# The tail of a one-core trunk kernel: three additions to x by VectorE in place of accumulating DMAs, squares moved behind sigmoids, two rows finished in parts

## The chip, the cores and the metric

The kernel runs on one core of one Trainium2 chip. The time is device microseconds (us) from one launch; lower is better. Five engines matter: TensorE (PE, matmul), VectorE (DVE), ScalarE (ACT), GpSimd (POOL) and SyncE (SP). Each executes its own instructions strictly in the order in which they were written down, and waits at an instruction until the semaphores that it names have been reached. DMAs are issued from SP and from POOL.

## The reference

One layer of a transformer trunk, batch 1, 512 tokens of width 2048, float32:

```python
hn = rmsnorm(x, norm_g[0])
y = swa_mixer(hn, w_in, w_out, sinks, rel_bias)   # windowed attention, gated, times w_out
x = x + y
emb = p[0] @ ple_proj[0]
g = jax.nn.sigmoid(rmsnorm(x, ple_norm[0]) @ ple_gate[0])
x = x + emb * g
return rmsnorm(x, final_g)                        # x * rsqrt(mean(x*x) + eps) * final_g
```

Only the last three lines concern the change: the sigmoid gate, the addition to x, and the final norm over each token's 2048 values.

## The kernel before

**Tiling.** x lies in SBUF as one tile `x1s` of 128 partitions x 4 column pieces j x 4 token rows t x 512, and `x1[j]` is its column piece j. The text names a piece of 128 tokens by 512 columns as (t, j); row t is the four pieces (t, 0) to (t, 3). Each matrix product is done with three float32r matmuls (high by high, low by high, high by low part: `mm3`), and the weights are split into the two parts by ACT (a cast, lines 755 and 763) and DVE (a subtraction, lines 756 and 764). The two large products (by `w_out`, then by `ple_gate`) are done by a two-level scheme of seven block products, worked in the order 1, 7, 6, 5, 3, 4. Product 5 yields the gate inputs of pieces (2, 2), (3, 2), (2, 3), (3, 3); product 3 those of (0, 2), (1, 2) and then (0, 3), (1, 3); the sums of several products those of (0, 0), (1, 0), (0, 1), (1, 1); product 4, which is last, those of (2, 0), (2, 1), (3, 0), (3, 1).

**Per piece** the generator `gated` (line 1381) writes three steps, and the caller decides by `next` and `run` where each lands: (a) a sigmoid on ACT, with the row's first norm as its scale (line 1387); (b) a multiplication by the embedding on DVE (line 1389), then the addition to x, either as a DMA issued from POOL with an add on arrival (line 1393) or as an addition on DVE (line 1395); (c) a square on ACT that also sums the 512 values into `ssq3` (line 1406). Step (c) reads the x that step (b) has made, so after a DMA it waits for that DMA to land.

**Per row**, once its four sums are there, `power_of_mean` makes the row's factor: a reduction and a scaling on DVE, a power on POOL (line 1361). The row is then multiplied by that factor and by the final gain, in one of two ways: in one DVE instruction (`row`, line 1420), or by the gain beforehand on DVE (`by_gain`, line 1412) and by the factor on ACT (line 1609 or 1621). `store` issues the piece's write to HBM from SP (line 1415).

**What sets the order.** For this stretch the order of all five engines is written by hand: the order of calls is the order on each engine. `later`, `moved` and `moves` are lists of steps: at fixed points between matmuls some of `later` is run; `moved` holds step (c) of gates whose DMAs are in flight, to be run at a later point.

**The tail.** `block(jj, tb)` issues the 24 matmuls of product 4 for piece (2 + tb, jj). PE works (2, 0), (2, 1), (3, 0) and then (3, 1) in two column parts of 288 and 224. `two` are the gates of (0, 3) and (1, 3). The last part of (3, 1) is squared and summed in one DVE instruction, row 3's factor follows on POOL, then the last scalings and stores. Tiles in the profile: `g` and `open` are PSUM banks with gate inputs, `s` the gate's scratch, `e` the embedding, `fg` the gain, `yn` the rows' factors.

Of the kernel before, what the change touches and what calls it, by code (L numbers as in the profile page):

```python
# [55 lines left out]
def trunk_kernel(ctx: ExitStack, tc: tile.TileContext, a: dict):  # L56
    nc = tc.nc
# [100 lines left out]
    def run(gen):  # L158
        for _ in gen:
            pass  # L160
# [21 lines left out]
    kinds, g = [], 0  # L182
# [16 lines left out]
    for k in range(KC):  # L199
# [95 lines left out]
        if 3 <= k < 3 + NB:  # L295
            t = k - 3
# [384 lines left out]
    def block(nm, r, c, jj, m):  # L681

        r = r if nm == "w_out" else 3 - r
        return a[nm][2 * (c - 1) + jj, 4 * (r - 1) + m]
# [16 lines left out]
    for nm, p in SUMS:  # L701
        for q in (6, 5) if (nm, p) == ("ple_gate", 5) else (p,):
            sum_small(nm, q)
        for jj in range(2):
            for m in range(4):
                t = summed[nm, p, jj, m] = tc.dram_tile([P, WE], F32, name=f"{nm}_{p}_{jj}_{m}")
# [262 lines left out]
    x1 = [x1s[:, j] for j in range(4)]  # L969
# [335 lines left out]
    for n, p in enumerate(ORDER_OUT):  # L1305
        nxt = out_forms.steps(ORDER_OUT[n + 1]) if n < 5 else iter(())
        for jj in range(2):
# [12 lines left out]
            def todo():  # L1320
                step = next(calls)
                part = x_at.get((p, jj, step))
                if part is not None:
                    load_x(part, nc.sync)
                part = embed_steps.get((p, jj, step))
                if part is not None:
                    embedding.prepare(part)
                next(nxt, None)
                if p == 4:

                    for _ in range({0: 1, 1: 2, 2: 2, 3: 2, 5: 1, 6: 2, 7: 2}.get(4 * jj + step, 0)):
                        turn(*turns.pop(0), "o")
                    if jj:
                        next(ple_first, None)
# [20 lines left out]
    def power_of_mean(out, ssq, nm):  # L1355

        w = out.shape[-1]
        ms = const.tile([P, NB], F32, tag="ms_r", name=f"ms_{nm}")[:, :w]
        nc.vector.tensor_scalar(ms, ssq, 1.0 / D, EPS, op0=ALU.mult, op1=ALU.add)
        yield  # L1360
        nc.gpsimd.tensor_tensor(out, ms, power[:, :w], op=ALU.pow)
# [7 lines left out]
    def load_embeds(c, jj):  # L1369
        t = embed_of[c, jj] = late.tile([P, 2, 512], F32, tag="e", name=f"e{c}_{jj}", bufs=2)  # L1370
        nc.sync.dma_start(t, embeds[c, jj])
# [9 lines left out]
    def gated(t, j, zin, z, e, c=slice(0, 512), share=1.0):  # L1381


        n = done[t]
        done[t] += 1
        xt = x1[j][:, t, c]
        nc.scalar.activation(z, zin, AF.Sigmoid, scale=rstd2[:, t : t + 1])
        yield
        nc.vector.tensor_mul(z, e[:, c], z)
        if t < 3 or j >= 2:  # L1390
            if t < 2 and j < 2:
                yield
            nc.gpsimd.dma_start(xt, z, accum_op=ALU.add)
        else:
            nc.vector.tensor_add(xt, xt, z)
        yield
        if (t, j) == (3, 1) and share != 1.0:
            flat = x1s.rearrange("p j t c -> p (j t c)")
            at = (NB + 3) * 512
            xt = flat[:, at + c.start : at + c.stop + 1]  # L1400
            nc.vector.scalar_tensor_tensor(
                out=s2[:, 1, 1, c.start - 1 : c.stop], in0=xt, scalar=share, in1=xt, op0=ALU.mult, op1=ALU.mult,
                accum_out=ssq3[:, t, n : n + 1],
            )
        else:
            nc.scalar.activation(z, xt, AF.Square, accum_out=ssq3[:, t, n : n + 1])

    def gain(j):
        return fg[:, j * 512 : (j + 1) * 512]

    def by_gain(t, j):
        nc.vector.tensor_mul(x1[j][:, t, :], x1[j][:, t, :], gain(j))

    def store(t, j):
        nc.sync.dma_start(a["out"][t * P : (t + 1) * P, j * 512 : (j + 1) * 512], x1[j][:, t, :])

    def row(t, j, yn):

        xt = x1[j][:, t, :]
        nc.vector.scalar_tensor_tensor(out=xt, in0=xt, scalar=yn, in1=gain(j), op0=ALU.mult, op1=ALU.mult)  # L1420
# [33 lines left out]
    moved, moves = [], []  # L1454
# [14 lines left out]
    opens = {  # L1469
        (3, 1, 0): (0, 0, "t"), (3, 1, 1): (1, 0, "t"), (3, 1, 2): (0, 1, "o"), (3, 1, 3): (1, 1, "o", lower),  # L1470
    }
    gains = {(3, 1, 0): (0, 0), (3, 1, 1): (1, 0), (3, 1, 2): (0, 1), (3, 1, 3): (1, 1)}

    def split_last(k):
        if k % 2 == 0:
# [16 lines left out]
    for n, p in enumerate(ORDER_PLE[:-1]):  # L1492
        if n == 1:

            ctx.enter_context(
                tc.manual_schedule(
                    engines={getattr(mybir.EngineType, v) for v in ("PE", "SP", "DVE", "Activation", "Pool")}
                )
            )
        nxt = ple_forms.steps(ORDER_PLE[n + 1])  # L1500
        for jj in range(2):
            calls = iter(range(4))

            def todo():
                step = next(calls)
                k = early.get((p, jj, step))
                if (p, jj, step) in embed_loads:
                    load_embeds(*embed_loads[p, jj, step])
                while small_due:
                    small_due.pop(0)()  # L1510
                if (p, jj, step) == (5, 0, 2):
                    assert len(moves) == 4
                    while moves:
                        moves.pop(0)()
                if turns:
                    turn(*turns.pop(0), "t")
                    if not turns:
                        nc.vector.tensor_reduce(ss2, ssq2, axis=AX.X, op=ALU.add)
                        run(power_of_mean(rstd2, ss2, "r2"))
                        nc.scalar.activation(ss2[:, :1], ss2[:, :1], AF.Sigmoid)  # L1520
                    return
                next(nxt, None)
                if p == 1:
                    next(nxt, None)
                if k is not None:
                    split_last(k)
                if (p, jj, step) in opens:
                    open_bank(*opens[p, jj, step])
                if (p, jj, step) in gains:
                    by_gain(*gains[p, jj, step])  # L1530

            def between(m, ps):
                if (p, m) == (7, 3):
                    gate(p, jj, ps, None)
                q = ple_steps.get((p, jj, m))
                if q is not None:
                    small_ple.prepare(q)
                for q in SMALL["ple_gate"].get((p, jj), {}).get(m, ()):
                    small_ple.product(q)
                if (p, jj, m) == (6, 1, 1):  # L1540
                    later.append(partial_of(gate_later, "sum", 0, None, embeds_for(1, 0)))

            ps = unit(p, jj, at_ple, ple_forms, todo, between)
            last_two, held_e = (p, jj) == (3, 1), {}
            if not (p == 7 or last_two):
                later.insert(0, partial_of(gate_later, p, jj, ps, held_e))
            for of, which in EMBEDS.get((p, jj), ()):
                e = embeds_for(of, which)
                held_e.update(e)
                if of == 1:  # L1550
                    later.insert(1, partial_of(gate_later, "sum", which, None, dict(e)))
                    held_e.clear()
            if p == 5 or (p, jj) == (3, 0):
                while moved:
                    later.extend(moved.pop(0))
        run(nxt)
# [21 lines left out]
    two = gate(3, 1, ps, e)  # L1578
# [1 line left out]
        for g in two:  # L1580
            next(g)
    load_embeds(4, 1)
    for step in moved.pop():
        step()
    yn2 = const.tile([P, 3], F32, name="yn2")
    ssum = const.tile([P, 3], F32, name="ssum")
    nc.gpsimd.memset(power[:, 3:], 0.5)
    first = block(0, 0)
    next(first)
    next(first)  # L1590
    for t in (2, 3):
        for j in (2, 3):
            by_gain(t, j)
    for g in two:
        run(g)
    nc.vector.tensor_reduce(ssum[:, :2], ssq3[:, :2, :4], axis=AX.X, op=ALU.add)
    root = power_of_mean(yn2[:, :2], ssum[:, :2], "r3")
    next(root)
    run(root)
    g = block(1, 0)  # L1600
    next(g)
    next(g)
    run(first)
    for t in range(2):
        for j in (2, 3):
            row(t, j, yn2[:, t : t + 1])
            store(t, j)
        for j in range(2):
            nc.scalar.mul(x1[j][:, t, :], x1[j][:, t, :], yn2[:, t : t + 1])
            store(t, j)  # L1610
    run(g)
    nc.vector.tensor_reduce(ssum[:, 2:], ssq3[:, 2, :4], axis=AX.X, op=ALU.add)
    root = power_of_mean(yn2[:, 2:], ssum[:, 2:], "r4")
    next(root)
    run(root)
    g = block(0, 1)
    next(g)
    next(g)

    def scaled_row(j):  # L1620
        nc.scalar.mul(x1[j][:, 2, :], x1[j][:, 2, :], yn2[:, 2:])

    scaled_row(2)
    for j in range(2):
        row(2, j, yn2[:, 2:])
    for j in (2, 0, 1):
        store(2, j)
    run(g)

    base, yn = (const.tile([P, 1], F32, name=f"{v}_3") for v in ("base", "yn"))  # L1630
    g = block(1, 1, lower)
    next(g)
    scaled_row(3)
    store(2, 3)
    next(g)
    by_gain(3, 0)
    run(g)
# [82 lines left out]
```

## Time and profile before

| | us |
|---|---|
| median of 3 runs (791.64 to 792.34) | 791.79 |
| the profiled execution's own time | 791.74 |
| its span, first to last instruction | 790.0 |
| PE busy | 777.2 (98%) |
| DVE busy | 609.0 (77%) |
| ACT busy | 525.7 (67%) |
| POOL busy | 151.6 (19%) |

The span is what the trace covers; 1.74 us of the profiled execution lie outside it. Busy shares are means over the whole span; the change touches only about its last 40 us, so those are read from the timeline there. In the timeline a row has the start in us, the duration in us, the engine, the line, the operation, output and input with their sizes, how many equal instructions were merged into it, and, in brackets, how long the engine was idle before it and what it was waiting for.

### The profile page before, as it was taken

The page shows a single profiled execution, that of the slowest core. Times are in us where ns is not written, and L with a number is a line of the kernel's source. Part 1 is how long each engine was busy: PE and PEld are TensorE (multiplying, and loading weights), DVE is VectorE, ACT ScalarE, POOL GpSimd, SP SyncE. Part 2 cuts the span into 40 slices and gives each one's busy share as a digit, 9 for nine tenths or more (in the row PEclk, how much of TensorE's full clock was granted, in tenths as well). Part 3 has the DMA queues.
Part 4 walks back from the last instruction along what each step waited for, and adds up shares of the span by engine and source line. Part 5 has one row for each costly group of instructions (what it writes and reads, how often), then busy time and mean ns, then how long its engine had stood idle before and what let it go on. Part 6 is the DMA issues. An engine that isn't in the chain of part 4 may idle for free. (4 is left out here: it accounts for less than half of the span.)

```text
span 790.0 us, 11176 instructions
## 1 busy us (share of the span) xinstructions
PE 777.2 (98%) x3708; PEld 649.5 (82%) x3708; DVE 609.0 (77%) x1046; ACT 525.7 (67%) x1105; POOL 151.6 (19%) x276
## 2 busy tenths in 40 slices
PE   9999999999999999999999999999999999999993
PEld 8888888888888888888888888888888888888783
DVE  4547697876878687877777898975897849998975
ACT  6743576666767586766666754568778967665964
POOL 0201423132223323122222200011000002221121
PEclk9999999999999999999999999999999999999997
DMA  9988899999999989999997489767797289999956
GB/s 345 279 219 297 190 277 300 296 276 266 279 264 273 264 232 316 236 306 263 274 268 192 137 319 356 238 239 243 263 391 251 80 322 277 271 274 323 262 121 226
DMA packets 50825, 207.51 MB, mean 263 GB/s; under 512 B 7552, under 2 KB 8576, under 8 KB 45008
## 3 DMA queue, kind: packets, MB, share of 16 engines
q1 hardware_dynamic: 39152, 154.58, 55.7%
q0 software_dynamic: 11616, 52.23, 32.9%
q8 instruction: 29, 0.48, 0.2%
q14 instruction: 28, 0.23, 0.1%
HBM read 192.31 MB, written 75.55 MB: 339 GB/s over the span
## 5 line engine op out<-in xcount | busy, mean ns | idle before, releaser
L756 DVE TENSOR_TENSOR blo<-braw,bhi 128x1024 fp32r<-128x1024 f32 x100 | 121.9, 1222 | 31.1 <-ACT bhi L755 30.2
L755 ACT CAST bhi<-braw 128x1024 fp32r<-128x1024 f32 x100 | 104.9, 1049 | 38.6 <-PE o L128 13.9
L126 PE MATMUL gps<-xh,whi 128*128 128x512 f32 x256 | 100.0, 390 | 0.0
L127 PE MATMUL gps<-xl,whi 128*128 128x512 f32 x256 | 99.9, 390 | 0.0
L128 PE MATMUL gps<-xh,wlo 128*128 128x512 f32 x256 | 99.7, 390 | 0.0
L126 PE MATMUL qps<-xh,whi 128*128 128x512 f32 x224 | 87.8, 392 | 0.0
L127 PE MATMUL qps<-xl,whi 128*128 128x512 f32 x224 | 87.4, 390 | 0.0
L128 PE MATMUL qps<-xh,wlo 128*128 128x512 f32 x224 | 87.3, 390 | 0.0
L570 POOL TENSOR_SCALAR_AFFINE_SELECT own<-r 64x512 fp32r<-64x512 f32 (+1 forms) x48 | 32.5, 676 | 243.4 <-DVE r L560 240.9
L110 DVE TENSOR_TENSOR wlo<-wraw,whi 128x1024 fp32r<-128x1024 f32 x60 | 73.5, 1226 | 3.4 <-ACT whi L109 3.2
L127 PE MATMUL o<-blo,fho 128*128 128x512 f32 x192 | 74.9, 390 | 0.0
L126 PE MATMUL o<-bhi,fho 128*128 128x512 f32 x192 | 74.8, 390 | 0.0
L128 PE MATMUL o<-bhi,flo 128*128 128x512 f32 x192 | 74.8, 389 | 0.0
L556 ACT CAST r<-pt 128x256 fp32r<-128x256 f32 x64 | 23.9, 374 | 68.9 <-PE pt L551 68.7
L109 ACT CAST whi<-wraw 128x1024 fp32r<-128x1024 f32 x60 | 62.3, 1040 | 5.2 <-issue 4.1
L126 PE MATMUL g<-bhi,fhg 128*128 128x512 f32 x160 | 62.8, 392 | 0.0
L127 PE MATMUL g<-blo,fhg 128*128 128x512 f32 x160 | 62.5, 391 | 0.0
L128 PE MATMUL g<-bhi,flg 128*128 128x512 f32 x160 | 62.3, 390 | 0.0
L128 PEld LDWEIGHTS gps<-xh,wlo 128*128 128x128 f32 x256 | 48.1, 188 | 10.3
L126 PEld LDWEIGHTS gps<-xh,whi 128*128 128x128 f32 x256 | 48.1, 188 | 9.1
L529 ACT ACTIVATE t<-t,sm 128x129 f32<-128x129 f32 (+1 forms) x128 | 49.6, 390 | 8.7 <-DVE sm L525 7.4
L560 DVE TENSOR_TENSOR r<-pt,r 128x256 fp32r<-128x256 f32 x56 | 23.7, 424 | 41.1 <-ACT r L556 40.4
(288 smaller groups left out, 1833.8 us busy)
## 6 DMA issues: line engine op xcount, KB each, us to landing
wraw<-in_w_gate_in SPq DMA_DIRECT2D x32, 512.0 KB, 7.9
w_out<-in_w_out POOLq DMA_DIRECT2D x32, 512.0 KB, 9.0
braw<-w_out SPq DMA_DIRECT2D x32, 512.0 KB, 5.2
wraw<-in_w_q SPq DMA_DIRECT2D x28, 512.0 KB, 6.6
braw<-in_w_out SPq DMA_DIRECT2D x22, 512.0 KB, 4.7
braw<-in_ple_gate SPq DMA_DIRECT2D x22, 512.0 KB, 6.5
xw<-in_first SPq DMA_DIRECT2D x14, 640.5 KB, 6.5
w_out<-in_w_out SPq DMA_DIRECT2D x16, 512.0 KB, 10.5
```

Of the source, the lines that this page charges most:

```text
L109: nc.scalar.copy(hi, raw)
L110: nc.vector.tensor_sub(lo, raw, hi.bitcast(F32))
L126: nc.tensor.matmul(ps, sh, mh, start=first, stop=False, skip_group_check=more)
L127: nc.tensor.matmul(ps, sh, ml, start=False, stop=False, skip_group_check=more)
L128: nc.tensor.matmul(ps, sl, mh, start=False, stop=last, skip_group_check=more)
L529: nc.scalar.activation(su, su, AF.Exp, bias=sm[:, u : u + 1], accum_out=sm[:, 2 + u : 3 + u])
L556: nc.scalar.copy(rh, src)
L560: nc.vector.tensor_sub(rl, src, rh.bitcast(F32))
L570: nc.gpsimd.affine_select(out=flat(own), in_=flat(r).bitcast(F32), pattern=[[0, 8], [sign, HB]], compare_op=ALU.is_ge, fill=0.0, base=-HB ...
L755: nc.scalar.copy(hi[:, :n], raw)
L756: nc.vector.tensor_sub(lo[:, :n], raw, hi[:, :n].bitcast(F32))
```

## The change

Nothing before the end of product 5 is touched, and PE's instructions are the same in the same order.

- Pieces (0, 3), (1, 3) and (2, 1) are added to x by DVE instead of a DMA from POOL. (3, 0) and (3, 1) were already added by DVE; (0, 2), (1, 2) and (2, 0) stay with the DMA.
- The squares of (2, 3) and (3, 3) are no longer run among the casts during product 3's second half, and the squares of (0, 2) and (1, 2) no longer before the sigmoid of (2, 0). The former are now behind the sigmoids of (0, 3) and (1, 3), the latter behind the sigmoid of (2, 0). The square of (2, 0) is now behind the sigmoid of (2, 1).
- The four multiplications by the gain of (0, 0), (1, 0), (0, 1), (1, 1) no longer stand among the weight splits of product 3 but in the tail; those of (2, 2), (2, 3) and of (3, 2), (3, 3) stand behind the row factors' reductions.
- Rows 0 and 1 are multiplied and stored in two parts, row 0 before row 1, around the second and third `block`; row 2's pieces (2, 2) and (2, 3) are multiplied by ACT after the third.

The core of the diff:

```diff
@@ gated
-        if t < 3 or j >= 2:
+        if (t >= 2) == (j >= 2) or (t, j) in ((0, 2), (1, 2), (2, 0)):
@@ loop over product 3
-    gains = {(3, 1, 0): (0, 0), (3, 1, 1): (1, 0), (3, 1, 2): (0, 1), (3, 1, 3): (1, 1)}
...
-                if (p, jj, step) in gains:
-                    by_gain(*gains[p, jj, step])
...
-            if p == 5 or (p, jj) == (3, 0):
+            if p == 5:
                 while moved:
                     later.extend(moved.pop(0))
@@ tail
-    for step in moved.pop():
+    for step in moved.pop(0):
         step()
...
+    def rows_by_gain(t):
+        for j in (2, 3):
+            row(t, j, yn2[:, t : t + 1])
+            store(t, j)
+
+    def rows_by_root(t, js):
+        for j in js:
+            nc.scalar.mul(x1[j][:, t, :], x1[j][:, t, :], yn2[:, t : t + 1])
+            store(t, j)
+
+    run(two[0])
+    by_gain(0, 0)
     first = block(0, 0)
     next(first)
     next(first)
-    for t in (2, 3):
-        for j in (2, 3):
-            by_gain(t, j)
-    for g in two:
-        run(g)
+    run(two[1])
+    for step in moved.pop(0):
+        step()
+    assert not moved
+    for t, j in ((1, 0), (0, 1), (1, 1)):
+        by_gain(t, j)
     nc.vector.tensor_reduce(ssum[:, :2], ssq3[:, :2, :4], axis=AX.X, op=ALU.add)
     root = power_of_mean(yn2[:, :2], ssum[:, :2], "r3")
     next(root)
     run(root)
+    for j in (2, 3):
+        by_gain(2, j)
     g = block(1, 0)
     next(g)
+    rows_by_gain(0)
     next(g)
+    rows_by_root(0, range(2))
+    rows_by_gain(1)
     run(first)
-    for t in range(2):
-        for j in (2, 3):
-            row(t, j, yn2[:, t : t + 1])
-            store(t, j)
-        for j in range(2):
-            nc.scalar.mul(x1[j][:, t, :], x1[j][:, t, :], yn2[:, t : t + 1])
-            store(t, j)
     run(g)
+    rows_by_root(1, range(2))
     nc.vector.tensor_reduce(ssum[:, 2:], ssq3[:, 2, :4], axis=AX.X, op=ALU.add)
     root = power_of_mean(yn2[:, 2:], ssum[:, 2:], "r4")
     next(root)
     run(root)
+    for j in (2, 3):
+        by_gain(3, j)
+    for j in range(2):
+        row(2, j, yn2[:, 2:])
+        store(2, j)
     g = block(0, 1)
     next(g)
     next(g)
-
-    def scaled_row(j):
-        nc.scalar.mul(x1[j][:, 2, :], x1[j][:, 2, :], yn2[:, 2:])
-
-    scaled_row(2)
-    for j in range(2):
-        row(2, j, yn2[:, 2:])
-    for j in (2, 0, 1):
-        store(2, j)
+    rows_by_root(2, (2, 3))
     run(g)
...
     g = block(1, 1, lower)
     next(g)
-    scaled_row(3)
-    store(2, 3)
     next(g)
     by_gain(3, 0)
     run(g)
```

What that makes of the instruction streams is seen best at two places. The first is ACT from the sigmoids of (0, 3) and (1, 3) to the sigmoid of (3, 0). Line 1387 is a sigmoid, and the bank it reads names the piece: `open0_0`, `open1_0`, `open0_1` are (2, 0), (2, 1), (3, 0), and `g1_1_0`, `g1_1_1` are (0, 3), (1, 3). Line 1406 is a square; a wait for DMASW is a wait for one of POOL's DMAs to land, one for DVE, PE or Pool is for that engine. Lines 1609 and 1593 multiply by a row factor. Before:

```order
L1406 ACTIVATE s1_5036,ssq3_5035<-x1s_5033 128x512 [waits DMASW1_49,DVE_49]
L1406 ACTIVATE s1_5036,ssq3_5035<-x1s_5033 128x512 [waits DMASW2_49,DVE_49]
L1387 ACTIVATE s2_5037<-open0_0_0_7687,rstd2_6603 128x512 [waits PE_49]
L1406 ACTIVATE s1_5036,ssq3_5035<-x1s_5033 128x512 [waits DMASW3_49,DVE_49]
L1406 ACTIVATE s1_5036,ssq3_5035<-x1s_5033 128x512 [waits DMASW4_49,DVE_49]
L1387 ACTIVATE s2_5037<-open1_0_0_7714,rstd2_6603 128x512 [waits PE_49,Activation_49]
L1406 ACTIVATE s2_5037,ssq3_5035<-x1s_5033 128x512 [waits DMASW5_49,DVE_49]
L1609 ACTIVATE x1s_5033<-x1s_5033,yn2_7777 128x512 [waits Pool_49]
L1609 ACTIVATE x1s_5033<-x1s_5033,yn2_7777 128x512 x3
L1406 ACTIVATE s2_5037,ssq3_5035<-x1s_5033 128x512 [waits DMASW6_49,DVE_49]
L1387 ACTIVATE s2_5037<-open0_1_0_7736,rstd2_6603 128x512 [waits PE_49,Activation_49]
```

The six squares are those of (0, 2), (1, 2), then (0, 3), (1, 3), then (2, 0), then (2, 1); the sigmoids of (2, 0), (2, 1) and (3, 0) stand behind two, two and one wait for a DMA. Now:

```order
L1406 ACTIVATE s7_5038,ssq3_5035<-x1s_5033 128x512 [waits DMASW7_49]
L1406 ACTIVATE s7_5038,ssq3_5035<-x1s_5033 128x512 [waits DMASW0_49]
L1406 ACTIVATE s1_5036,ssq3_5035<-x1s_5033 128x512 [waits DVE_49]
L1387 ACTIVATE s2_5037<-open0_0_0_7687,rstd2_6603 128x512 [waits PE_49]
L1406 ACTIVATE s1_5036,ssq3_5035<-x1s_5033 128x512 [waits DVE_49]
L1406 ACTIVATE s1_5036,ssq3_5035<-x1s_5033 128x512 [waits DMASW1_49]
L1406 ACTIVATE s1_5036,ssq3_5035<-x1s_5033 128x512 [waits DMASW2_49]
L1387 ACTIVATE s2_5037<-open1_0_0_7713,rstd2_6603 128x512 [waits PE_49,Activation_49]
L1593 ACTIVATE x1s_5033<-x1s_5033,yn2_7771 128x512 [waits Pool_49]
L1593 ACTIVATE x1s_5033<-x1s_5033,yn2_7771 128x512 [waits DVE_49]
L1406 ACTIVATE s2_5037,ssq3_5035<-x1s_5033 128x512 [waits DMASW3_49]
L1406 ACTIVATE s2_5037,ssq3_5035<-x1s_5033 128x512 [waits DVE_49]
```

The squares are those of (2, 3), (3, 3), (0, 3), then behind the sigmoid (1, 3), (0, 2), (1, 2), then behind the next sigmoid and row 0's two multiplications (2, 0) and (2, 1). Two multiplications of row 1 and the sigmoid of (3, 0) follow.

The second place is DVE from the last weight split (line 764) to the second row factor's reduction. Line 1412 is a multiplication by the gain, 1420 a row piece by factor and gain, 1395 an addition to x. Before:

```order
L764 TENSOR_TENSOR low7_7762<-grown93_6975,last6_7755 128x1024 [waits DMASW0_49,DVE_49,Activation_49]
L1389 TENSOR_TENSOR s1_5036<-e3_1_7708,s1_5036 128x512 [waits DMAHW5_49,Activation_49]
L1389 TENSOR_TENSOR s1_5036<-e3_1_7708,s1_5036 128x512 [waits Activation_49]
L1389 TENSOR_TENSOR s2_5037<-e4_0_7753,s2_5037 128x512 [waits DMAHW6_49,Activation_49]
L1412 TENSOR_TENSOR x1s_5033<-x1s_5033,fg_6241 128x512 [waits DMASW5_49]
L1412 TENSOR_TENSOR x1s_5033<-x1s_5033,fg_6241 128x512 [waits DMASW7_49]
L1412 TENSOR_TENSOR x1s_5033<-x1s_5033,fg_6241 128x512 [waits DMASW6_49]
L1412 TENSOR_TENSOR x1s_5033<-x1s_5033,fg_6241 128x512 [waits DMASW0_49]
L1596 TENSOR_REDUCE ssum_7778<-ssq3_5035 128x2 [waits Activation_49]
L1359 TENSOR_SCALAR ms_r3_7814<-ssum_7778 128x2 [waits DVE_49,Pool_49]
L1389 TENSOR_TENSOR s2_5037<-e4_1_7773,s2_5037 128x512 [waits DMAHW7_49,Activation_49]
```

Now:

```order
L764 TENSOR_TENSOR low7_7756<-grown93_6975,last6_7750 128x1024 [waits DMASW0_49,DVE_49,Activation_49]
L1389 TENSOR_TENSOR s1_5036<-e3_1_7707,s1_5036 128x512 [waits DMAHW5_49,Activation_49]
L1395 TENSOR_TENSOR x1s_5033<-x1s_5033,s1_5036 128x512 [waits DVE_49]
L1389 TENSOR_TENSOR s1_5036<-e3_1_7707,s1_5036 128x512 [waits Activation_49]
L1395 TENSOR_TENSOR x1s_5033<-x1s_5033,s1_5036 128x512 [waits DVE_49]
L1412 TENSOR_TENSOR x1s_5033<-x1s_5033,fg_6241 128x512 [waits DMASW1_49]
L1389 TENSOR_TENSOR s2_5037<-e4_0_7748,s2_5037 128x512 [waits DMAHW6_49,Activation_49]
L1412 TENSOR_TENSOR x1s_5033<-x1s_5033,fg_6241 128x512 [waits DMASW2_49]
L1412 TENSOR_TENSOR x1s_5033<-x1s_5033,fg_6241 128x512 [waits DMASW3_49]
L1412 TENSOR_TENSOR x1s_5033<-x1s_5033,fg_6241 128x512 [waits DMASW4_49]
L1607 TENSOR_REDUCE ssum_7772<-ssq3_5035 128x2 [waits Activation_49]
L1359 TENSOR_SCALAR ms_r3_7810<-ssum_7772 128x2 [waits DVE_49,Pool_49]
```

Two additions and four multiplications by the gain (one, then three) now stand between the last weight split and the reduction, where four others stood, and no multiplication by the gain stands among the weight splits any more. On POOL the DMAs of (0, 3), (1, 3) and (2, 1) are gone from between the others.

## The prediction

> Times are us from the span's start in the profiled execution before.
>
> **What bounds the kernel now.** I read the busy table by windows first, then the timeline of PE, then ACT's waits, and last the chain of waits, which here needs care.
>
> ```profile
> 760.00:770.00 10.00, 10.00 (x46) 8.29 (x45) 5.33 (x10) 4.03 (x11) 2.70 (x5) 1.00 0.87 176
> 761.02 0.39 PE L128 MATMUL open<-last,flg 128*128 128x512 f32 x1
> 766.46 0.39 PE L128 MATMUL open<-last,flg 128*128 128x512 f32 x1
> 771.90 0.39 PE L128 MATMUL open<-last,flg 128*128 128x512 f32 x1
> 775.15 0.30 PE L128 MATMUL open<-last,flg 128*128 128x288 f32 x1
> 777.84 0.27 PE L128 MATMUL open<-last,flg 128*128 128x224 f32 x1
> ```
>
> In the window PE is busy all the 10 us at full clock (the second number and the 1.00). The five PE rows are the last matmuls of (2, 0), (2, 1), (3, 0) and of the two parts of (3, 1): they end at 761.41, 766.85, 772.29, 775.45 and 778.11, and PE is then done. The span is 790.0, so 11.9 us follow. The sigmoids that wait for these ends start much later:
>
> ```profile
> 763.75 0.67 ACT L1387 ACTIVATE s<-open,rstd 128x512 f32<-128x512 f32 x1
> 767.38 0.63 ACT L1406 ACTIVATE s<-x1s 128x512 f32<-128x512 f32 x1 [2.96 <-DMA x1s<-s]
> 768.71 0.63 ACT L1406 ACTIVATE s<-x1s 128x512 f32<-128x512 f32 x1 [0.61 <-DMA x1s<-s]
> 769.34 0.67 ACT L1387 ACTIVATE s<-open,rstd 128x512 f32<-128x512 f32 x1
> 775.90 0.63 ACT L1406 ACTIVATE s<-x1s 128x512 f32<-128x512 f32 x1 [2.59 <-DMA x1s<-s]
> 776.53 0.67 ACT L1387 ACTIVATE s<-open,rstd 128x512 f32<-128x512 f32 x1
> 779.32 0.48 ACT L1387 ACTIVATE s<-open,rstd 128x288 f32<-128x288 f32 x1
> 780.87 0.44 ACT L1406 ACTIVATE s<-x1s 128x288 f32<-128x288 f32 x1 [0.46 <-DVE x1s L1395]
> 781.32 0.43 ACT L1387 ACTIVATE s<-open,rstd 128x224 f32<-128x224 f32 x1
> ACT s L1406 <- DMA x1s<-s: 9.2, 5, 3.0
> ```
>
> The five sigmoids (L1387) come 2.34, 2.49, 4.24, 3.87 and 3.21 behind their matmuls. Ahead of each of the first three stands a square (L1406) that waits for a DMA to land: ACT is idle 9.2 us in five such waits (last row: total, times, longest). The delay then runs in a ring: late sigmoid, late multiplication, late DMA, late square, next sigmoid late.
>
> ```profile
> 777.66 4.27 issue
> 782.07 0.38 DVE L1389 TENSOR_TENSOR s<-e,s 128x224 f32<-128x224 f32 x1
> ```
>
> The chain of waits doesn't name this: it begins with 4.27 us of "issue" on POOL, time for which it found no releaser. What ends last is the upper part of (3, 1): sigmoid 781.32, multiplication 782.07, and from there 7.93 to the end. PE would have allowed that sigmoid at 778.15:
>
> ```profile
> 707.38 0.39 PE L128 MATMUL g<-bhi,flg 128*128 128x512 f32 x1
> 707.81 1.05 ACT L755 CAST bhi<-braw 128x1024 fp32r<-128x1024 f32 x1 [1.67 <-PE g L128]
> ```
>
> where ACT waits for PE, it starts 0.04 after the matmul's end. So the most that reordering can win is what lies between 778.15 and 781.32, and a little on DVE.
>
> **Part 1: the weight splits.** Four multiplications by the gain leave DVE and two squares leave ACT from before the last splits.
>
> ```profile
> 751.32 0.68 DVE L1412 TENSOR_TENSOR x1s<-x1s,fg 128x512 f32<-128x512 f32 x1
> 759.48 1.21 DVE L764 TENSOR_TENSOR low<-grown,last 128x1024 fp32r<-128x1024 f32 x1
> 760.61 1.28 DVE L1389 TENSOR_TENSOR s<-e,s 128x512 f32<-128x512 f32 x2
> 758.13 1.25 ACT L1387 ACTIVATE s<-g,rstd 128x512 f32<-128x512 f32 x2
> 765.06 2.49 DVE L1412 TENSOR_TENSOR x1s<-x1s,fg 128x512 f32<-128x512 f32 x4
> 770.75 2.74 DVE L1420 SCALAR_TENSOR_TENSOR x1s<-x1s,yn,fg 128x512 f32<-128x512 f32 x4
> 777.24 0.69 DVE L1389 TENSOR_TENSOR s<-e,s 128x512 f32<-128x512 f32 x1 [0.23 <-ACT s L1387]
> 777.96 0.69 DVE L1395 TENSOR_TENSOR x1s<-x1s,s 128x512 f32<-128x512 f32 x1
> ```
>
> Instructions overlap a little: four gains take 2.49, so 0.60 each behind one another; four row pieces 2.74, so 0.67; an addition that needs the multiplication before it starts 0.72 after it. DVE reaches the multiplication of (0, 3) 4 x 0.60 = 2.4 earlier, 758.2. ACT saves two squares of 0.63, sigmoids at about 756.9. PE gets its splits earlier, never later; as it has no gap to close, that is worth nothing in itself.
>
> **Part 2: (0, 3) and (1, 3) on DVE.** Two multiplications, two additions and one gain from 758.2: 0.72, 0.60, 0.72, 0.60, 0.69, free at 761.5. ACT does the deferred squares of (2, 3), (3, 3) (landed long before) and that of (0, 3) by 760.3 and is free for the sigmoid of (2, 0) at 761.45, where it was at 763.75.
>
> **Part 3: the one DMA that still matters.** The multiplication of (2, 0) runs 762.15 to 762.85.
>
> ```profile
> 764.45 0.69 DVE L1389 TENSOR_TENSOR s<-e,s 128x512 f32<-128x512 f32 x1 [2.56 <-ACT s L1387]
> 765.68 0.85 POOL L1393 DMA_DIRECT2D x1s<-s  x1 [2.25 <-issue]
> DMA to landing us min/median/max: 4.2/4.2/4.2
> DMA to landing us min/median/max: 4.2/5.9/6.7
> DMA to landing us min/median/max: 4.0/6.0/10.5
> 763.12 0.63 ACT L1406 ACTIVATE s<-x1s 128x512 f32<-128x512 f32 x1 [0.54 <-DMA x1s<-s]
> ```
>
> The same DMA now starts 0.54 after its multiplication's end, so 763.4 then. The three landing rows are for this one DMA, for the six of the tail, for all fourteen of this line. I take 4.2, its own row: 767.6. The bounds are 4.0 and 10.5. The last row is the square of (1, 2), whose data landed at 763.1; its DMA is issued no later now, and its square comes third behind the sigmoid of (2, 0), at 763.3. No wait.
>
> **Part 4: rows 0 and 1.** Behind the multiplication of (2, 0) DVE does three gains, to 764.6.
>
> ```profile
> 776.66 0.16 DVE L1612 TENSOR_REDUCE ssum<-ssq 128x1 f32<-128x4 f32 x1 [3.17 <-ACT s L1406]
> 777.09 0.56 POOL L1361 TENSOR_TENSOR yn<-ms_r,power 128x1 f32<-128x1 f32 x1 [4.91 <-DVE ms_r L1359]
> ```
>
> From reduction to the end of the power is 0.99: factors at 765.6, where DVE has two gains to do anyway, to 766.2, then two pieces of row 0 to 767.5. The sigmoid of (2, 1) is due at 766.89 and ends at 767.56 (was 769.34); multiplication 767.6, addition 768.3 to 769.0, two pieces of row 1 to 770.25. ACT: row 0's multiplications to 768.8, square of (2, 0) there (landed 767.6), square of (2, 1) 769.4 to 770.15. Reduction at 770.25, gains to 771.8 (the factor is there at 771.3), two pieces of row 2 to 773.1.
>
> ```profile
> 761.92 0.32 SPq L1371 DMA_DIRECT2D e<-embeds  x1
> DMA to landing us min/median/max: 2.4/3.5/4.8
> ```
>
> On SP the last embedding's load (first row) waits for the multiplication of (1, 3), so it goes out at 760.2 and has 7.4 until the multiplication of (2, 1). Behind it come the stores, in the order in which rows are now finished, from about 767 on, each 256 KB and landed within 2.4 to 4.8 (second row, all fourteen). Nothing on another engine waits for a store except POOL's power ahead of the last square, which overwrites one value of the stored (0, 2): it has 10 us.
>
> **Part 5: row 3.** The sigmoid of (3, 0) runs 772.33 to 773.0; its multiplication waits for DVE till 773.1, addition 773.8 to 774.5, square to 775.15. The lower sigmoid is due at 775.49: 0.34 spare. Before, 1.55 passed from it to its square (779.32, 780.87) and 0.45 more to the upper sigmoid: square 777.04, ACT free 777.5, upper sigmoid at PE's 778.15. Its multiplication follows 0.43 + 0.04 later, 778.62; DVE's work between the lower square and that point took 1.20 (780.87 to 782.07), so it is free at 778.24: 0.38 spare.
>
> **Sum.** 782.07 - 778.62 = 3.45 earlier; the 7.93 behind it are the same instructions and transfers. Profiled 791.74 - 3.45 = 788.29; the median of the runs is 0.05 above the profiled execution: 788.3.
>
> DVE costs nothing extra as long as the spare 0.34 + 0.38 = 0.72 and the waits for sigmoids cover it: three additions (2.1) and four gains (2.4) come in, against 2.4 earlier and 2.56 of waiting that it had at 764.45. Without that cover each further us of DVE would be a us at the end.
>
> **A rule against it.** POOL's power now runs beside gains on DVE:
>
> ```profile
> 769.99 0.72 POOL L1361 TENSOR_TENSOR yn<-ms_r,power 128x2 f32<-128x2 f32 x1 [3.46 <-DVE ms_r L1359]
> 770.04 0.69 DVE L1389 TENSOR_TENSOR s<-e,s 128x512 f32<-128x512 f32 x1
> ```
>
> The two ran together before, and DVE's 0.69 is its usual 0.69. If they excluded each other, each of the two factors would come one gain later and push the next gain by the power's 0.6: 0.7 twice, 1.4 in all on DVE, less the spare 0.72: 0.7 lost. The Trainium skill ("SBUF — State Buffer", "Who interferes with whom") says just this: a VectorE instruction with two SBUF inputs and a GpSimd instruction that reads SBUF exclude each other, and the second waits for the first's end. By that rule the time is 789.0; the pair of rows above speaks against it.
>
> **Rivals.** *Exclusion on POOL and DVE*, as priced: 789.0. For it: both factors stand beside gains. Against it: the rows at 769.99 and 770.04.
>
> *The DMA of (2, 0) lands late*, and ACT, in order, holds row 1, the sigmoids of (3, 0) and (3, 1) behind its square. It is needed at 768.8, and with 0.1 at the reduction and the spare 0.72 nothing is lost up to 769.6, 6.2 after its start. At 6.7 it costs 0.5: 788.8. At 9.65 the whole gain is gone. At 10.5 the kernel is slower than before: 773.9 - 769.6 - 3.45 = 0.85, 792.6. For it: one of the fourteen took that long, and new stores start at 767. Against it: by itself it took 4.2, and the six of the tail never above 6.7.
>
> *Another end.* What I don't see, an output transfer or a wait that holds the end where it is: 791.8.
>
> **How the numbers follow.** My forecast 0.74 (its own range 787.4 to 789.2, as the last transfers may land up to a us sooner or later, by the range of the stores); exclusion 0.09; late DMA 0.12, of which 0.05 still faster by over 0.2% (1.6 us, about what a measurement here tells from no change), 0.04 within it, 0.03 slower; another end 0.05, 0.02 within and 0.03 slower. Faster 0.88, same 0.06, slower 0.06. Range 787.4 to 790.3: a late DMA of up to 8.2 is inside.
>
> **What would show it.** Right: the five sigmoids of line 1387 within 0.1 of 761.45, 766.9, 772.3, 775.5, 778.15; no wait of ACT on a DMA from 755 on; PE unchanged to its end. Wrong: a wait before the square of (2, 0); the upper sigmoid behind 778.4 with DVE busy without a gap before it; a power on POOL above 1 us; or the sigmoids on time and more than 7.93 behind the last multiplication.

## The result, and the profile after

The changed kernel takes 787.99 us (median of 6 runs, 787.38 to 788.25), the kernel before beside it 791.68 (6 runs, 791.07 to 792.34): 0.9953 of the time, with a 95% interval of 0.9940 to 0.9966, or 3.7 us less. The profiled execution took 788.25 with a span of 786.5, where 790.0 - 3.45 = 786.55 was forecast.

First the line of busy times of the changed kernel's page, and from its table of windows the stretch from 760 to 770 (length, then busy time and count of PE, weight loads, DVE, ACT, POOL, then PE's clock, share of the DMA engines, GB/s):

```profile
PE 777.0 (99%) x3708; PEld 649.9 (83%) x3708; DVE 611.3 (78%) x1049; ACT 525.5 (67%) x1105; POOL 150.3 (19%) x273
760.00:770.00 10.00, 10.00 (x46) 8.29 (x45) 9.37 (x17) 6.16 (x17) 1.95 (x2) 1.00 0.63 168
```

PE is as full as before. DVE went from 5.33 (10 instructions) to 9.37 (17) in this stretch and ACT from 4.03 (11) to 6.16 (17), since they stand still less and work of the rows that came after 770 now falls in it, on DVE additions and gains too; the DMA engines went from 0.87 to 0.63. The five sigmoids and the squares of (2, 0) and (3, 0), from the timeline of ACT, with the row of ACT's waits that now stands where the 9.2 us on DMAs stood, and PE's last matmul:

```profile
761.32 0.69 ACT L1387 ACTIVATE s<-open,rstd 128x512 f32<-128x512 f32 x1 [0.86 <-PE open L128]
766.82 0.69 ACT L1387 ACTIVATE s<-open,rstd 128x512 f32<-128x512 f32 x1 [2.98 <-PE open L128]
768.64 0.62 ACT L1406 ACTIVATE s<-x1s 128x512 f32<-128x512 f32 x1
772.26 0.69 ACT L1387 ACTIVATE s<-open,rstd 128x512 f32<-128x512 f32 x1 [1.07 <-PE open L128]
774.44 0.63 ACT L1406 ACTIVATE s<-x1s 128x512 f32<-128x512 f32 x1 [0.27 <-DVE x1s L1395]
775.42 0.50 ACT L1387 ACTIVATE s<-open,rstd 128x288 f32<-128x288 f32 x1 [0.26 <-PE open L128]
778.09 0.45 ACT L1387 ACTIVATE s<-open,rstd 128x224 f32<-128x224 f32 x1 [0.61 <-PE open L128]
ACT s L1387 <- PE open L128: 5.8, 5, 3.0
777.72 0.27 PE L128 MATMUL open<-last,flg 128*128 128x224 f32 x1
```

Each of the five now waits for PE and for nothing else (brackets: idle time before it, and what ended it), and the square of (2, 0) at 768.64 follows without a wait. The rest of the tail, from the timelines of DVE and POOL and the view of this one DMA:

```profile
762.05 0.69 DVE L1389 TENSOR_TENSOR s<-e,s 128x512 f32<-128x512 f32 x1 [0.41 <-ACT s L1387]
763.27 0.86 POOL L1393 DMA_DIRECT2D x1s<-s  x1 [6.08 <-issue]
DMA to landing us min/median/max: 3.4/3.4/3.4
764.80 1.29 DVE L1412 TENSOR_TENSOR x1s<-x1s,fg 128x512 f32<-128x512 f32 x2
764.98 1.09 POOL L1361 TENSOR_TENSOR yn<-ms_r,power 128x2 f32<-128x2 f32 x1 [0.85 <-DVE ms_r L1359]
770.47 1.28 DVE L1412 TENSOR_TENSOR x1s<-x1s,fg 128x512 f32<-128x512 f32 x2
770.63 0.92 POOL L1361 TENSOR_TENSOR yn<-ms_r,power 128x1 f32<-128x1 f32 x1 [4.56 <-DVE ms_r L1359]
778.57 0.39 DVE L1389 TENSOR_TENSOR s<-e,s 128x224 f32<-128x224 f32 x1 [0.35 <-ACT s L1387]
```

The last multiplication starts at 778.57 (before: 782.07), and 786.5 - 778.57 = 7.93 follow, as before; in all thirteen profiles of this document it is between 7.89 and 7.98, though the first store starts at 771.53 before and at 766.88 in the change. So neither the earlier stores nor another end is what the gain hangs on. PE's end moves from execution to execution: its last matmul started between 776.85 and 778.08 in the profiles below. So I compare the *tail*, the span less the start of that matmul: 790.0 - 777.84 = 12.16 before, 786.5 - 777.72 = 8.78 after. Spans are printed to a tenth, so a tail is good to about 0.05.

### The profile page after: what moved, and what is told of

The parts are those of the page before. It is cut to its first block, busy times and chain, and to the rows that moved or that the text cites. A ratio compares the mean times of both kernels' runs of the same rounds, so it can differ in the third digit from the quotient of the medians.

```text
span 786.5 us, 11166 instructions
## 1 busy us (share of the span) xinstructions
PE 777.0 (99%) x3708; PEld 649.9 (83%) x3708; DVE 611.3 (78%) x1049; ACT 525.5 (67%) x1105; POOL 150.3 (19%) x273
## 4 chain that ended last, share of the span: by engine, by line
PE 93%; DMA 2%; DVE 1%; issue 1%; ACT 1%; POOL 0%; POOLq 0%; DVEq 0%; ACTq 0%
PE gps L126 7%; PE gps L127 7%; PE gps L128 7%; PE qps L126 7%; PE qps L127 7%; PE qps L128 7%; PE o L127 6%; PE o L126 6%; PE o L128 6%; PE g L127 3%; PE g L128 3%; PE g L126 3%; DMA braw<-ple_gate 2%; PE s L485 2%; PE vps L290 2%; PE pt L551 2%
```

## The experiments

Every run has a kernel before beside it on the same chip; its median was 791.65 beside the first four, 792.13 beside the next four, 791.44 beside the last three.

| kernel | median us (runs) | ratio to before, 95% interval | tail |
|---|---|---|---|
| before | 791.68 (6) | 1 | 12.16 |
| the change | 787.99 (6) | 0.9953, 0.9940 to 0.9966 | 8.78 |
| e1 the additions alone | 788.18 (4) | 0.9956, 0.9941 to 0.9971 | 8.75 |
| e2 the order alone | 797.59 (4) | 1.0071, 1.0056 to 1.0086 | 18.12 |
| e3 gains early again | 787.69 (4) | 0.9951, 0.9936 to 0.9966 | 8.79 |
| e4 squares early again | 788.61 (5) | 0.9962, 0.9948 to 0.9976 | 9.32 |
| e5 one more on DVE | 787.90 (4) | 0.9943, 0.9928 to 0.9958 | 8.75 |
| e6 three more on DVE | 788.98 (4) | 0.9958, 0.9943 to 0.9973 | 10.02 |
| e7 no DMA left | 788.12 (4) | 0.9947, 0.9932 to 0.9962 | 8.79 |
| e8 the DMA of (2, 0) late | 790.98 (10) | 0.9987, 0.9977 to 0.9996 | 11.91 |
| e9 gains ahead of the reductions | 788.07 (3) | 0.9957, 0.9941 to 0.9973 | 9.39 |
| e10 before, (2, 1) on DVE | 788.76 (5) | 0.9971, 0.9957 to 0.9985 | 9.58 |
| e11 before, (0, 3), (1, 3) on DVE | 788.42 (4) | 0.9963, 0.9948 to 0.9978 | 8.86 |

The intervals are about 1.2 us to each side, so medians tell apart only before, e2, e8 and the rest. Differences of some tenths among the rest are read from tails, of one profiled execution each; the five kernels in which the last sigmoid waits for PE (the change, e1, e3, e5, e7) lie between 8.75 and 8.79.

**e1, the additions alone.** The kernel before, with the change's condition and nothing else of it:

```diff
-        if t < 3 or j >= 2:
+        if (t >= 2) == (j >= 2) or (t, j) in ((0, 2), (1, 2), (2, 0)):
```

> The kernel before with one line of the change: (0, 3), (1, 3) and (2, 1) are added by VectorE, all orders as before. Theory (ScalarE's in-order waits for landing DMAs form a ring, and the end follows the upper sigmoid of (3, 1)): the squares of (0, 2), (1, 2) still hold the sigmoid of (2, 0) to about 763.7, but those of (0, 3), (1, 3) and (2, 1) wait for nothing; only the square of (2, 0) waits, to about 770, and row 0's and 1's four multiplications stand behind it. Upper sigmoid about 778.6, its multiplication about 779.3, 2.8 us faster than before, about 0.75 slower than the change. Rival A (the shares of the parts simply add up, additions and order about half each): 1.7 faster. Rival B (the earlier output stores are what counts): no difference from before.

It took the whole gain: tail 8.75, where I had expected 0.75 more than the change. Its stores are issued in the order of before, so their new order is not what counts. From its timelines of ACT and POOL, and its waits:

```profile
763.26 0.67 ACT L1387 ACTIVATE s<-open,rstd 128x512 f32<-128x512 f32 x1
765.19 0.86 POOL L1393 DMA_DIRECT2D x1s<-s  x1 [7.78 <-issue]
768.56 0.63 ACT L1406 ACTIVATE s<-x1s 128x512 f32<-128x512 f32 x1 [1.11 <-DMA x1s<-s]
772.26 0.67 ACT L1387 ACTIVATE s<-open,rstd 128x512 f32<-128x512 f32 x1
778.02 0.45 ACT L1387 ACTIVATE s<-open,rstd 128x224 f32<-128x224 f32 x1 [0.62 <-PE open L128]
ACT s L1406 <- DMA x1s<-s: 3.8, 3, 2.1
```

Three waits on DMAs, 3.8 us, are still there, and the sigmoid of (2, 0) is nearly 2 us later than in the change. Yet the last sigmoid waits for PE: the DMA of (2, 0) starts 1.9 later but lands 3.4 behind its start, and ACT does the square when the change does, at 768.56. The lateness is gone before the end.

**e2, the order alone.** The change with the old condition:

```diff
-        if (t >= 2) == (j >= 2) or (t, j) in ((0, 2), (1, 2), (2, 0)):
+        if t < 3 or j >= 2:
```

> The change with its additions undone: its whole order, but (0, 3), (1, 3) and (2, 1) added by DMAs again. Theory: the square of (0, 3) now stands ahead of the sigmoid of (2, 0) and waits for its DMA to about 764, and that of (2, 1) stands ahead of row 1's multiplications and of the sigmoid of (3, 0) and waits to about 776; upper multiplication about 784, 1 to 3 us SLOWER than before. Rival A (shares add up): 1.7 faster than before. Rival B (stores): faster by most of 3.5.

It is slower than before, by about 6 us. Its timelines of POOL and ACT, and its waits:

```profile
759.65 1.74 POOL L1393 DMA_DIRECT2D x1s<-s  x2 [2.20 <-DVE s L1389]
766.21 0.63 ACT L1406 ACTIVATE s<-x1s 128x512 f32<-128x512 f32 x1 [7.09 <-DMA x1s<-s]
766.84 0.67 ACT L1387 ACTIVATE s<-open,rstd 128x512 f32<-128x512 f32 x1
774.67 0.90 POOL L1393 DMA_DIRECT2D x1s<-s  x1 [2.59 <-issue]
779.95 0.63 ACT L1406 ACTIVATE s<-x1s 128x512 f32<-128x512 f32 x1 [5.90 <-DMA x1s<-s]
781.80 0.67 ACT L1387 ACTIVATE s<-open,rstd 128x512 f32<-128x512 f32 x1
ACT s L1406 <- DMA x1s<-s: 13.9, 3, 7.1
```

The moved squares cannot help: the one left ahead of the sigmoid of (2, 0) is that of (0, 3), whose DMA starts only at 759.65 and lands 6.5 later. ACT stands 7.09, the last 4.5 of it with the sigmoid due (PE's last matmul of (2, 0) ended at 761.65). That sigmoid is 5 us late (766.84), so the later DMA starts at 774.67 and its square holds the next sigmoid until 781.80. Two long waits and one of 0.96 stand in place of five shorter ones, and each feeds the next.

**e3 and e4, one move undone at a time.** In e3 the four gains go back among product 3's splits; in e4 the squares of (2, 3), (3, 3) go back among the casts and those of (0, 2), (1, 2) ahead of the sigmoid of (2, 0). The core of e3, then of e4:

```diff
+                if (p, jj, step) in gains:
+                    by_gain(*gains[p, jj, step])
...
-    by_gain(0, 0)
...
-    for t, j in ((1, 0), (0, 1), (1, 1)):
-        by_gain(t, j)
```

> The change with the four multiplications by the gain of (0, 0), (1, 0), (0, 1), (1, 1) back among the weight splits. Theory: the multiplication of (0, 3) is 2.4 later on VectorE (760.7), the sigmoid of (2, 0) about 1.3 later because the square of (0, 3) stands ahead of it, but three gains fewer follow, so VectorE is about 0.7 late at the multiplication of (3, 0), and its spare time there (0.6) swallows that: within 0.2 us of the change. Rival (clearing VectorE's queue among the splits is a part of the gain by itself): 1 to 2.4 us slower than the change.

```diff
-            if p == 5:
+            if p == 5 or (p, jj) == (3, 0):
...
     run(two[1])
-    for step in moved.pop(0):
-        step()
```

> The change with its four moved squares back: (2, 3), (3, 3) among the casts, (0, 2), (1, 2) ahead of the sigmoid of (2, 0). Theory: the sigmoid of (2, 0) starts at about 762.5 in place of 761.3, VectorE is 1.2 late from there, less its spare 0.6: about 0.6 us slower than the change, still 2.9 faster than before. Rival A (shares add up): the squares carry 1 us or more. Rival C (squares that wait for nothing cost nothing wherever they stand): no difference from the change.

The move of the gains is worth nothing (8.79). The move of the squares is worth 9.32 - 8.78 = 0.54 within the change's order, though e1 does as well without it. In e4 the sigmoid of (2, 0) is late again, behind two squares that wait 1.5 for their DMAs. The lateness reaches the end, since DVE has the four gains in its tail and runs without a gap from 763.13 to 775.36; the last sigmoid follows ACT's work and not PE:

```profile
762.43 0.67 ACT L1387 ACTIVATE s<-open,rstd 128x512 f32<-128x512 f32 x1
777.97 0.43 ACT L1387 ACTIVATE s<-open,rstd 128x224 f32<-128x224 f32 x1
```

PE's last matmul started at 777.38 there, so this sigmoid was due at about 777.7.

**e5, e6 and e7: how much room DVE has.** e5 and e6 add one and three multiplications into scratch behind row 1's pieces by the gain; e7 takes the last DMA away too.

```diff
     rows_by_gain(1)
+    for _ in range(3):
+        nc.vector.tensor_mul(s7[:, 0, 0], gain(0), gain(1))
```

> The change with one more VectorE multiplication of 128x512 (0.60 us, into scratch) behind row 1's two pieces, where VectorE waits for nothing until the multiplication of (3, 0). The tail is measured from the start of PE's last matmul to the end of the span: 8.78 in the change. Theory (spare time of 0.61 on VectorE up to the upper multiplication): no cost, tail 8.8, sigmoid of (3, 1) lower up to 0.3 later. Rival D (VectorE is the bound now, its 0.94 busy share in 760 to 770 says so): 0.6 us slower, tail 9.4.

> The same with three such multiplications, 1.8 us. Theory: 1.8 less the spare 0.61, 1.2 us slower than the change, tail 10.0. Rival D: 1.8 slower, tail 10.6. Rival E (PE sets the end with room to spare): tail 8.8.

```diff
-        if (t >= 2) == (j >= 2) or (t, j) in ((0, 2), (1, 2), (2, 0)):
+        if (t >= 2) == (j >= 2) or (t, j) in ((0, 2), (1, 2)):
```

> The change with (2, 0) added by VectorE too, so that no DMA is left in the tail. Theory: the DMA of (2, 0) lands before its square is due, so nothing is gained, and the addition costs VectorE 0.7 behind the multiplication of (2, 0), which its spare time takes but for 0.1: tail 8.8 to 8.9. Rival (each addition taken from a DMA is worth about a third of 3.4): tail 7.6.

From e5's timelines of DVE and ACT:

```profile
769.34 0.68 DVE L1620 TENSOR_TENSOR s<-fg 128x512 f32<-128x512 f32 x1
769.95 0.15 DVE L1624 TENSOR_REDUCE ssum<-ssq 128x1 f32<-128x4 f32 x1
777.22 0.45 ACT L1387 ACTIVATE s<-open,rstd 128x224 f32<-128x224 f32 x1 [0.39 <-PE open L128]
```

and from e6's:

```profile
770.16 2.14 DVE L1620 TENSOR_TENSOR s<-fg 128x512 f32<-128x512 f32 x3
772.22 0.15 DVE L1624 TENSOR_REDUCE ssum<-ssq 128x1 f32<-128x4 f32 x1
776.45 0.63 ACT L1406 ACTIVATE s<-x1s 128x512 f32<-128x512 f32 x1 [1.51 <-DVE x1s L1395]
777.08 0.48 ACT L1387 ACTIVATE s<-open,rstd 128x288 f32<-128x288 f32 x1
779.02 0.43 ACT L1387 ACTIVATE s<-open,rstd 128x224 f32<-128x224 f32 x1
779.78 0.38 DVE L1389 TENSOR_TENSOR s<-e,s 128x224 f32<-128x224 f32 x1
```

One more pushes the reduction back by 769.95 - 769.34 = 0.61 and costs nothing; the last sigmoid still waits 0.39 for PE. Three push it by 2.06 (they write one tile and follow each other 0.72 apart), the wait for PE is gone, and the tail grows by 10.02 - 8.78 = 1.24. So DVE's room was 2.06 - 1.24 = 0.82, where the forecast had 0.72. My expectation for e6, 10.0, was met by luck: I had taken 1.8 for the three and 0.61 for the room, and both were 0.2 to 0.3 too small. e7 puts one addition more on DVE and takes the last DMA off POOL: 8.79, neither gain nor loss.

**e8, the DMA of (2, 0) issued late.** It goes out behind the first factor's power and four fills of scratch on POOL:

```diff
-            if t < 2 and j < 2:
+            if t < 2 and j < 2 or (t, j) == (2, 0):
                 yield
...
     run(root)
+    for _ in range(4):
+        nc.gpsimd.memset(s7[:, 0, 0], 0.0)
+    next(first)
```

> The change with the DMA of (2, 0) issued behind the first row factor and four memsets of 128x512 on POOL. Theory: its square holds ScalarE, and with it row 2's factor and everything of row 3, from the point at which the landing comes later than about 9.0 us before PE's last matmul (769.3 in the change's trace minus 0.6 spare taken in): each us later is a us at the end. So tail = 8.8 + (start of the square of (2, 0), counted from PE's last matmul, plus 8.4): a square 5.0 before the last matmul gives 12.2. Rival (row 2's factor is off the path): tail 8.8.

```profile
768.15 0.90 POOL L1393 DMA_DIRECT2D x1s<-s  x1
772.62 0.63 ACT L1406 ACTIVATE s<-x1s 128x512 f32<-128x512 f32 x1 [4.01 <-DMA x1s<-s]
780.79 0.43 ACT L1387 ACTIVATE s<-open,rstd 128x224 f32<-128x224 f32 x1
```

ACT waits 4.01 with the sigmoid of (3, 0) queued behind the square. The forecast's landing without cost was 769.6, that is 777.84 - 769.6 = 8.24 ahead of PE's last matmul. Here the square starts 777.59 - 772.62 = 4.97 ahead of it, 3.27 later, which gives 8.78 + 3.27 = 12.05, and by the limit in the expectation 12.2; measured 11.91. One late DMA gives most of the gain back: 3.13 of 3.38 by the tails, and by the medians of this group 790.98 against about 788 for the change (e5, e7) and 792.13 before, some 3 of 4.

**e9, gains ahead of the reductions.** So POOL's powers run beside no multiplication by the gain:

```diff
     for t, j in ((1, 0), (0, 1), (1, 1)):
         by_gain(t, j)
+    for j in (2, 3):
+        by_gain(2, j)
     nc.vector.tensor_reduce(ssum[:, :2], ssq3[:, :2, :4], axis=AX.X, op=ALU.add)
...
-    for j in (2, 3):
-        by_gain(2, j)
```

and the same with (3, 2) and (3, 3) at the second reduction.

> The change with the two pairs of multiplications by the gain, of (2, 2), (2, 3) and of (3, 2), (3, 3), put ahead of the two reductions instead of behind them, so that no two-input VectorE instruction runs beside POOL's two powers. In the change these powers took 1.09 and 0.92, before 0.72 and 0.56. Theory F (a VectorE instruction with two SBUF inputs holds back POOL's reads until it ends): the powers take 0.72 and 0.56 again. Rival (POOL's spans are rough, the longer ones are chance): 0.9 to 1.1 again. Time by the theory of the spare: the second factor comes 1.3 later for row 2, less 0.6: 0.7 us slower than the change, tail 9.5.

```profile
765.37 0.72 POOL L1361 TENSOR_TENSOR yn<-ms_r,power 128x2 f32<-128x2 f32 x1 [2.05 <-DVE ms_r L1359]
771.74 0.54 POOL L1361 TENSOR_TENSOR yn<-ms_r,power 128x1 f32<-128x1 f32 x1 [5.64 <-DVE ms_r L1359]
770.12 1.28 DVE L1412 TENSOR_TENSOR x1s<-x1s,fg 128x512 f32<-128x512 f32 x2
```

The powers take 0.72 and 0.54 here, and 1.09 and 0.92 in the change: there each is held up by 0.37 or 0.38. But the pairs of gains beside them take 1.29 and 1.28 in the change, and a pair with no power beside it takes 1.28 in e9 (last row): DVE is not held up. The tail is 0.61 longer in e9, as DVE now has to wait for both factors.

**e10 and e11, which addition it is.** The kernel before, with only (2, 1), or only (0, 3) and (1, 3), taken from the DMAs:

```diff
-        if t < 3 or j >= 2:
+        if (t < 3 or j >= 2) and (t, j) != (2, 1):
```

> The kernel before with only (2, 1) added by VectorE. Theory (ring of waits): the sigmoids of (2, 0) and (2, 1) stay late (763.7, 769.3) behind the squares of (0, 3), (1, 3); the square of (2, 1) no longer waits for a DMA but stands behind four multiplications, to 773.3; sigmoid of (3, 0) 774, upper multiplication about 1.0 later than with all three: tail 9.8, 2.4 us faster than before. Rival A (shares add up, a third each): tail 11.0, 1.1 faster.

```diff
-        if t < 3 or j >= 2:
+        if (t < 3 or j >= 2) and (t, j) not in ((0, 3), (1, 3)):
```

> The kernel before with only (0, 3) and (1, 3) added by VectorE. Theory: the sigmoid of (2, 1) is on time (766.9), the DMA of (2, 1) starts at about 768.7 and lands at 772.5 to 773.2, so its square and the sigmoid of (3, 0) come about 1 to 1.6 later than with all three, of which 0.6 is spare: tail 9.2 to 9.8, 2.4 to 3.0 us faster than before. Rival A: tail 9.9, 2.3 faster.

The first alone wins 12.16 - 9.58 = 2.58 of the tail, the other two alone 3.30, all three 3.41 (e1). From e10's timeline of ACT, then from e11's of POOL and ACT:

```profile
773.46 0.66 ACT L1387 ACTIVATE s<-open,rstd 128x512 f32<-128x512 f32 x1
778.24 0.43 ACT L1387 ACTIVATE s<-open,rstd 128x224 f32<-128x224 f32 x1
```

```profile
768.94 0.89 POOL L1393 DMA_DIRECT2D x1s<-s  x1
772.38 0.63 ACT L1406 ACTIVATE s<-x1s 128x512 f32<-128x512 f32 x1 [0.33 <-DMA x1s<-s]
778.01 0.45 ACT L1387 ACTIVATE s<-open,rstd 128x224 f32<-128x224 f32 x1
```

In e11 the DMA of (2, 1) starts at 768.94 and its square at 772.38, 3.44 later, after a wait of 0.33 only. Breaking the ring at either place lets it catch up almost to the end.

## Why the prediction was right, and where not

**What bounds it: right.** The ring of late sigmoid, late multiplication, late DMA and late square set the end. The five sigmoids came at 761.32, 766.82, 772.26, 775.42 and 778.09 for the forecast 761.45, 766.9, 772.3, 775.5 and 778.15. The first is 0.13 off where 0.1 was named, but PE's own end is 0.12 earlier here. No wait of ACT on a DMA was left, and e8 puts most of the lateness back with one late DMA.

**Sum: right.** 3.45 forecast; the upper multiplication came 782.07 - 778.57 = 3.50 earlier and the tail is 3.38 shorter. The 7.93 behind it held to within what a span shows. That the profiled execution came within 0.05 of the forecast is in part luck: it is the slowest of its six runs, and PE's end alone moves by up to 1.23 between the profiles.

**Part 1, the weight splits: right in size, credited too much.** That PE has no gap to close was said, and PE's end did not move by more than its spread. The gains' move is worth nothing (e3), and e1 reaches the same tail with the four gains and the squares at their old places. The sum was made along the one path of the finished order, and nothing in it asked which edits it needs. It needs the additions alone. Within the new order the moved squares are then worth 0.54 (e4). The parting of rows 0 and 1 was not undone by itself; with everything else of the order it adds nothing to e1 that shows.

**Part 2, (0, 3) and (1, 3) on DVE: right.** Its multiplication of (0, 3) started at 758.29 for 758.2, and the sigmoid of (2, 0) waited for PE.

**Part 3, the one DMA that still matters: a term mis-sized.** The landing was taken as 4.2 and was 3.4; the start was 763.27 for 763.4. So the data were there 0.9 earlier than forecast (766.7 for 767.6), with no effect on the end, as ACT comes to that square only at 768.6. But the same 0.8 is a good part of why I expected less of e1 and of e11 than they gave: there the DMA is on the path. The 4.2 was not that of the DMA by itself, as the forecast's rival has it: the DMA of (1, 3), started at 762.2, landed 6.4 later and was still in flight beside it. With that one gone it took 3.4, and 3.3 in e2, where six such DMAs are in the tail but none beside this one. That the neighbour is the cause was not tried by itself.

**Part 4, rows 0 and 1: right.** The second reduction came at 770.21 for 770.25 forecast.

**Part 5, row 3: right.** The room was forecast as 0.34 + 0.38 = 0.72. In the change's rows ACT is idle 0.26 ahead of the lower sigmoid and DVE 0.35 ahead of the last multiplication, 0.61 together, and e6 gives 0.82. The brackets count too little, since instructions that don't wait overlap. Where nothing waits for PE (e6), the lower sigmoid starts 0.63 behind the square (776.45, 777.08), in the change 0.98 (774.44, 775.42); the last multiplication starts 2.70 behind that sigmoid in e6 and 3.15 in the change. That is 0.35 + 0.45 = 0.80.

**A rule against it: the reason given bears on one half only, the forecast held.** I set the exclusion aside because of the rows at 769.99 and 770.04. In these the power had started first, so they show that DVE is not held up behind a power, and nothing for a power that starts second. The runs show that one held up: 1.09 and 0.92 beside gains, 0.72 and 0.54 without (e9), and the sign that I had named for it, a power above 1 us, is there. What was wrong in the rival's price is the other half: DVE lost nothing, and the factors were needed only after the two gains. So 0.7 was priced and nothing was paid. The Trainium skill ("SBUF — State Buffer", "Who interferes with whom") has a VectorE instruction with two SBUF inputs and a GpSimd instruction that reads SBUF exclude each other. By that rule POOL's power waits for the running gain to end, and the trace agrees: wherever the power of two values starts in a multiplication, it ends 0.58 or 0.59 behind that one's end (last section). The rule would also hold VectorE's next instruction behind the power, and there the runs speak against it: the multiplication at 770.04 kept its 0.69, and the pairs of gains took 1.29 and 1.28.

**The late DMA: a real mechanism that did not occur.** Its limit and its slope, taken together, were right within 0.14 at the one point tried (12.05 against 11.91 in e8); the DMA landed 3.4 after its start, where 6.2 were free.

**The chance for the order by itself.** The forecast did not price the moves without the additions. My expectation for e2 was far too small, because I added up single waits; in a ring each wait also starts the next DMA later, and ACT's total of waits on DMAs went from 9.2 to 13.9.

## What to carry to other kernels

An instruction that waits for a DMA and stands, on an engine that works in order, ahead of one that is due holds everything behind it: look in the list of waits for such pairs, and ask whether the late result feeds the next DMA. Where waits form a ring, their shares do not add, and breaking it at one place can win most of it (here 2.58 and 3.30 alone, 3.41 together); reordering without removing the DMA can lengthen it. Before crediting a bundle of edits, work the path out for the smallest of them alone, and do not size a transfer by its row of before where the transfers beside it will be gone (4.2 became 3.4 here).

## What the runs showed of the hardware

- A small GpSimd power that starts while VectorE runs a two-input multiplication is held up until that multiplication ends. For two values, the power takes 0.72 by itself. Started 0.02 behind the multiplication it took 1.25 (e1), 0.15 behind 1.13 (e11), 0.18 behind 1.09 (the change, with 0.69 for the first of the two gains). In all three it ended 0.58 or 0.59 behind the multiplication's end. The one that started 0.05 ahead of a multiplication (before, 769.99 and 770.04) took 0.72. VectorE's instructions kept their time in every case. Where in the chip the two meet no run here shows.
- A DMA that adds 256 KB to a tile landed in 3.3 or 3.4 us where it started with no other of its kind in flight and no store (the change; in e2 that of (2, 0), with as many such DMAs in the tail as before). It took 4.2 before, beside another of its kind; 4.4 in e8 and, for that of (2, 1), 5.2 in e2, where stores were under way; and 5.7 to 8.1 in the tails where two were issued one behind the other (before, e2, e10). That what is in flight is the cause was not tried by itself.

From e1's timeline, then from e11's, the powers that started within a multiplication:

```profile
767.48 0.69 DVE L1389 TENSOR_TENSOR s<-e,s 128x512 f32<-128x512 f32 x1
767.50 1.25 POOL L1361 TENSOR_TENSOR yn<-ms_r,power 128x2 f32<-128x2 f32 x1 [1.44 <-DVE ms_r L1359]
768.20 0.69 DVE L1395 TENSOR_TENSOR x1s<-x1s,s 128x512 f32<-128x512 f32 x1
```

```profile
767.68 0.69 DVE L1389 TENSOR_TENSOR s<-e,s 128x512 f32<-128x512 f32 x1
767.83 1.13 POOL L1361 TENSOR_TENSOR yn<-ms_r,power 128x2 f32<-128x2 f32 x1 [1.45 <-DVE ms_r L1359]
```

In e1 the addition behind the multiplication starts 0.72 after it, as ever.
